# One table for positions, frequencies and norms, and a sum of squares on ScalarE, at the start of a two-layer decoder trunk

## The chip, the cores and the metric

The kernel runs on one core of one Trainium2 chip. The metric is the device time of one execution in microseconds (us); what is compared is the median over several executions.

## The reference, cut to what matters

The reference is a trunk of two residual layers over 256 tokens of width 1024. Layer 0 has gated DeltaNet heads and block attention in parallel, layer 1 has latent attention, and both layers end with a PEER expert network. Each sub-layer starts with the same step, and the attention parts need rotary tables:

```
mod = cond @ mod_w[layer] + mod_b[layer]
sh1, sc1, g1, sh2, sc2, g2 = jnp.split(mod[:, None, :], 6, axis=-1)
h = rmsnorm(x, norm_mix[layer]) * (1.0 + sc1) + sh1
...
inv_freq = ROPE_THETA ** (-jnp.arange(0, dim, 2, dtype=jnp.float32) / dim)
ang = positions.astype(jnp.float32)[..., None] * inv_freq
return jnp.cos(ang), jnp.sin(ang)
```

So before the first product with the input projection `hy_w_in` can run, the kernel needs the sum of squares of each token, 16 columns' worth of `mod` at a time, and the first weights. The rotary tables are needed only later.

## The kernel before, in words

Tokens lie in two tiles of 128 (`TT` = 2), one token per partition. Matrix products run in float32r, each weight and each activation split into a high part (ScalarE, a cast, L132) and a low part (VectorE, a subtraction, L132), three matmuls per pair (L136 to L138).

The change touches the start of `run` (L1673 to L1757). For this stretch the order of SP's DMA issues, of TensorE, VectorE and ScalarE is the order in which the code is written (`in_order`, L1641); only GpSimd is ordered by the scheduler. The steps are:

- SP loads `cond`, the two tiles of `x` (L1677), then, in four rounds `q`, two pieces of the modulation weights `mod0` (`mw`, 1 MB each, L1687) and one piece of `w0start` (`wraw`, 1 MB, L783), the first weights of the input projection. All loads of this stretch go through SP's one queue. In round 0, between the first `mw` and the first `wraw`, stand the small loads: the table `small` with modulation biases and norm gains (L1725), and inside `sincos` (L879), called twice, the frequencies (L888, one DRAM row read for all 128 partitions) and the positions (L889).
- VectorE squares and sums both token tiles (L1714), then runs a chain of tiny operations for the reciprocal root (L202, L154 to L178); ScalarE and VectorE scale the tiles by it (L225, L223) and TensorE transposes them (L232).
- In each round VectorE multiplies modulation weights with the row of `cond` (L349), TensorE does one column of it as 16 one-column matmuls per round (L1693), ScalarE and VectorE split `wraw` (L132), and `quarter` (L276) makes two of the eight 128-row blocks of `hT`, scaled and shifted (L235 to L251). Then the products of that quarter follow (L136 to L138).
- `sincos` runs on GpSimd: positions to float (L891), angles (L893), range reduction (L900 to L909). ScalarE takes the sines much later (L910).

`square_sum` (L192) is an existing helper that squares and sums on ScalarE; later norms use it.

Of the kernel before, what the change touches and what calls it, by code (L numbers as in the profile page):

```python
# [13 lines left out]
I32 = mybir.dt.int32  # L14
U32 = mybir.dt.uint32
AF = mybir.ActivationFunctionType
OP = mybir.AluOpType
AX = mybir.AxisListType

P = 128  # L20
D = 1024
KD = D // P
S = 256
TT = S // P
# [43 lines left out]
class Trunk:  # L68
# [34 lines left out]
    def consts(self):  # L103
        nc, b = self.nc, self.base
        self.x = self.t(b, [P, TT, D])
        self.small = self.t(b, [P, 2 * 48 + 4 * KD])
        self.modb = self.small[:, :96].rearrange("p (l c) -> p l c", l=2)
        self.normc = self.small[:, 96:128].rearrange("p (n c) -> p n c", n=4)
        tmp = ExitStack()
        d = self.t(tmp.enter_context(self.pool("c0", side="right")), [P, P], I32)  # L110
        nc.gpsimd.iota(d, pattern=[[1, P]], base=0, channel_multiplier=-1)
        self.ident = self.t(b, [P, P])
        nc.vector.tensor_scalar(self.ident, d, 0.0, None, op0=OP.is_equal)
        self.causal = self.t(b, [P, P])
        nc.vector.tensor_scalar(self.causal, d, 0.0, NEG, op0=OP.is_gt, op1=OP.mult)
        self.upper = self.t(b, [P, P])
        nc.vector.tensor_scalar(self.upper, d, 0.0, None, op0=OP.is_ge)
        tmp.close()
        self.ones = self.t(b, [P, 1])
        nc.vector.memset(self.ones, 1.0)  # L120
        self.cs1 = self.t(b, [P, TT, 2, 32])
        self.modc = [self.t(b, [P, 48]) for _ in range(2)]
        self.row = self.t(b, [P, D])
        self.ss4, self.ss2 = self.t(b, [P, TT, 4]), self.t(b, [P, TT, 4])
        nc.vector.memset(self.ss4, 0.0)
        self.eps = self.t(b, [P, 4])
        nc.vector.memset(self.eps, RS * EPS / 4)
# [751 lines left out]
    def sincos(self, out, half, freq):  # L879

        nc = self.nc
        tmp = self.t(self.st, [P, D], tag="lo", bufs=2)
        w = TT * half
        ang, t, n, r0, r1 = (tmp[:, k * w:(k + 1) * w].rearrange("p (i f) -> p i f", i=TT) for k in range(5))
        f, pos, posf = (tmp[:, 5 * w + a:5 * w + b]
                        for a, b in ((0, half), (half, half + TT), (half + TT, half + 2 * TT)))
        pos = pos.bitcast(I32)
        nc.sync.dma_start(f, freq[None, :].to_broadcast([P, half]))  # L888
        nc.sync.dma_start(pos, self.a["pos"])  # L889
        ve = nc.gpsimd  # L890
        ve.tensor_copy(posf, pos)  # L891
        for i in range(TT):
            ve.tensor_scalar(ang[:, i], f, posf[:, i:i + 1], None, op0=OP.mult)  # L893
        c1 = 6.28125
        c2 = float((np.float32(2 * np.pi - c1).view(np.uint32) & np.uint32(0xFFFFF000)).view(np.float32))
        c3 = float(2 * np.pi - c1 - c2)
        magic = 12582912.0
        steps = []
        for j, (turn, add) in enumerate(((0.25, float(np.pi / 2)), (0.0, 0.0))):
            ve.tensor_scalar(n, ang, float(0.5 / np.pi), turn, op0=OP.mult, op1=OP.add)  # L900
            ve.tensor_scalar(n, n, magic, None, op0=OP.add)
            ve.tensor_scalar(n, n, -magic, None, op0=OP.add)
            r = (r0, r1)[j]
            for k, c in enumerate((c1, c2, c3)):
                ve.tensor_scalar(t, n, -c, None, op0=OP.mult)
                ve.tensor_tensor(r, t, r if k else ang, op=OP.add)
            lim = 3.1415925
            ve.tensor_scalar(r, r, add, lim, op0=OP.add, op1=OP.min)
            ve.tensor_scalar(r, r, -lim, None, op0=OP.max)  # L909
            steps.append(lambda j=j, r=r: nc.scalar.activation(out[:, :, j], r, AF.Sin))  # L910
        return steps
# [722 lines left out]
    def run(self, out):  # L1634
        nc = self.nc
# [30 lines left out]
        r = Bag()  # L1666
        with self.pool("hc") as hc:
# [7 lines left out]
            nc.sync.dma_start(cond, self.a["condc"])  # L1675
            for i in range(TT):
                nc.sync.dma_start(self.x[:, i], self.a["x"][i * P:(i + 1) * P])  # L1677
            nc.scalar.activation(cond, cond, AF.Silu)
            self.row_of(self.row, cond)
            with self.pool("mod") as mp, start:  # L1680
# [3 lines left out]
                def mods(q, c, pm=None):  # L1684

                    w = self.t(mp, [P, 2, D], tag="mw", bufs=6)
                    nc.sync.dma_start(w, self.a["mod0"][q, c // 8])  # L1687
                    self.mod_tile(0, c, w[:, 0])
                    if pm is None:
                        self.mod_tile(0, c + 1, w[:, 1])  # L1690
                        return
                    for k in range(KD):
                        nc.tensor.matmul(pm[:, c // 8:c // 8 + 1], w[:, 1, k * P:(k + 1) * P], cond[:, k:k + 1],  # L1693
                                         start=k == 0, stop=k == KD - 1)
# [12 lines left out]
                def products(q, cs):  # L1707
                    for c in cs:
                        for j in range(2):
                            product(sums[c], c, j, w, q)  # L1710

                for i in range(TT):
                    sq = self.t(mp, [P, D], tag="sq")
                    nc.vector.scalar_tensor_tensor(sq, self.x[:, i], 1.0, self.x[:, i], op0=OP.mult, op1=OP.mult,  # L1714
                                                   accum_out=self.ss4[:, i, :1])
                e.norm(0, 1)
                e.turn(0, (0,))
                e.turn(1, (0,))
# [1 line left out]
                w = None  # L1720
                for q in range(4):
                    pm = self.ps()
                    mods(q, 8 + 2 * q, pm)
                    if not q:
                        nc.sync.dma_start(self.small, self.a["small"])  # L1725
                        turns = self.sincos(r.cs, 64, self.a["freq_b"]) + self.sincos(self.cs1, 32, self.a["freq_c"])
                    else:
                        products(q - 1, (1, 2, 3))
                    if q < 3:
                        w, steps = self.fetch(self.a["w0start"][q], KD, 256)  # L1730
                        for f in steps:
                            f()
                    mods(q, 2 * q)
                    bias(2 * q)
                    bias(8 + 2 * q, pm)
                    if q == 3:
                        w, steps = self.fetch(self.a["w0start"][q], KD, 256, 4)
                    last = e.quarter(q, tmp)
                    if q < 3:
                        products(q, (0,))  # L1740
                    if q == 1:
                        e.turn(0, (1,))
                        e.turn(1, (1,))
# [58 lines left out]
def _layout(i):  # L1802

    def f(n):
        return np.asarray(i[n])
# [12 lines left out]
    def cols(v):  # L1818
        return v.reshape(v.shape[:-1] + (-1, P)).swapaxes(-1, -2)

    def start(c, natural):
        w = f("mod_w")[0, :, c * P:(c + 2) * P]
        b = w[:, P:]
        return np.stack([w[:, :P].T, b.reshape(KD, P, P).swapaxes(0, 1).reshape(P, -1) if natural else b.T], 1)

    L = 2
    hy = f("hy_w_in")[0]
    wq = f("peer_w_q").reshape(L, KD, P, 8, 256).transpose(0, 3, 2, 1, 4).reshape(L, 8, P, 2048)
    uq = f("mla_w_uq")[0].reshape(512, 8, 192)
# [2 lines left out]
    w0 = chunks(np.concatenate([hy[:, :1536], hy[:, 2056:], hy[:, 1536:2048]], 1), 256)  # L1832
    r = {
        "x": f("x")[0],
        "pos": f("positions")[0].reshape(TT, P).T,
        "modT": f("mod_w").transpose(0, 2, 1),
        "condc": cols(f("c")[0]),
        "mod0": np.stack([np.stack([start(c, c >= 8) for c in (2 * q, 8 + 2 * q)]) for q in range(4)]),
        "small": np.concatenate([cols(f("mod_b")).transpose(1, 0, 2).reshape(P, -1)]
                                + [cols(f(n)[l]) for l in range(L) for n in ("norm_mix", "norm_ffn")], 1),  # L1840
        "w0": w0,
        "w0start": w0[[2, 3, 10, 11]].reshape(4, P, 4, 512).transpose(2, 1, 0, 3).reshape(4, P, 2048),
        "w0ba": one(hy[:, 2048:2056]),
# [11 lines left out]
        "wq": wq,  # L1855
        "keys": f("peer_sub_keys").reshape(L, 16, NK, P).transpose(0, 3, 1, 2),
        "uT": f("peer_u").reshape(L, NK, NK, KD, P).transpose(0, 2, 4, 3, 1).reshape(L, NK, P, D),
        "v": f("peer_v"),
        "final_norm": f("final_norm"),
    }  # L1860
    for n, d in (("freq_b", 128), ("freq_c", 64)):
        r[n] = np.power(np.float32(10000.0), -np.arange(0, d, 2, dtype=np.float32) / np.float32(d)).astype(np.float32)
    return {k: np.ascontiguousarray(v) for k, v in r.items()}


# [15 lines left out]
```

## Time and profile before

| what | value |
|---|---|
| median of 3 runs | 1913.13 us (1910.81 to 1915.3) |
| the profiled execution, its own time | 1913.58 us |
| span of the profile | 1911.8 us |
| TensorE busy | 1878.6 us, 98% of the span |
| VectorE busy | 1532.3 us, 80% |
| ScalarE busy | 943.5 us, 49% |
| GpSimd busy | 48.9 us, 3% |
| mean DMA rate over the span | 196 GB/s |

The profiled execution takes 1.8 us longer than its span; that part lies outside the instructions of the engines. Shares of busy time are averages over the whole span. The change lies in the first 50 us, so the rows that matter are those of that stretch.

### The profile page before, as it was taken

The page shows a single profiled execution, that of the slowest core. Times are in us where ns is not written, and L with a number is a line of the kernel's source. Part 1 is how long each engine was busy: PE and PEld are TensorE (multiplying, and loading weights), DVE is VectorE, ACT ScalarE, POOL GpSimd, SP SyncE. Part 2 cuts the span into 40 slices and gives each one's busy share as a digit, 9 for nine tenths or more (in the row PEclk, how much of TensorE's full clock was granted, in tenths as well). Part 3 has the DMA queues.
Part 4 walks back from the last instruction along what each step waited for, and adds up shares of the span by engine and source line. Part 5 has one row for each costly group of instructions (what it writes and reads, how often), then busy time and mean ns, then how long its engine had stood idle before and what let it go on. Part 6 is the DMA issues. An engine that isn't in the chain of part 4 may idle for free.

```text
span 1911.8 us, 35995 instructions
## 1 busy us (share of the span) xinstructions
PE 1878.6 (98%) x14368; PEld 1722.2 (90%) x14368; DVE 1532.3 (80%) x3265; ACT 943.5 (49%) x1301; POOL 48.9 (3%) x131
## 2 busy tenths in 40 slices
PE   6999999999999999999999999999999999999998
PEld 6999899999999888888889899999999988888886
DVE  7879789999998789865657677999778878985565
ACT  2866555454444444454545754545444444444453
POOL 7001000000000000000000000000000000000000
PEclk9999999999999999999999999999999999999999
DMA  8456475658885555576743455565555555556673
GB/s 324 160 194 214 191 279 187 201 187 284 295 270 187 177 177 177 176 251 195 216 147 111 155 201 175 183 203 186 180 175 170 176 177 176 176 180 199 194 228 103
DMA packets 96504, 374.57 MB, mean 196 GB/s; under 512 B 11856, under 2 KB 12112, under 8 KB 89680
## 3 DMA queue, kind: packets, MB, share of 16 engines
q1 hardware_dynamic: 96336, 372.28, 58.4%
q8 instruction: 112, 1.84, 0.4%
q14 instruction: 56, 0.46, 0.1%
HBM read 371.18 MB, written 1.05 MB: 195 GB/s over the span
## 4 chain that ended last, share of the span: by engine, by line
PE 82%; DVE 9%; DMA 4%; ACT 3%; issue 1%; SPq 0%; ACTq 0%; DVEq 0%
PE ps L776 30%; PE ps L621 21%; PE ps L623 11%; PE ps L136 3%; PE ps L138 3%; PE ps L137 3%; PE ps L644 3%; DVE lo L132 3%; DMA raw<-in_v_dram 2%; PE ps L729 1%; DVE t L349 1%; PE ps L324 1%; ACT hi L132 1%; PE ps L1200 1%; DVE wlo L132 1%
## 5 line engine op out<-in xcount | busy, mean ns | idle before, releaser
L132 ACT CAST hi<-raw 128x1024 fp32r<-128x1024 f32 x508 | 534.8, 1054 | 753.1 <-PE ps L776 310.5
L132 DVE TENSOR_TENSOR lo<-raw,hi 128x1024 fp32r<-128x1024 f32 x508 | 620.0, 1222 | 249.0 <-ACT hi L132 246.8
L621 PE MATMUL ps<-hT,hi 128*128 128x256 f32 x4096 | 514.2, 278 | 0.0
L621 PEld LDWEIGHTS ps<-hT,hi 128*128 128x128 f32 x4096 | 485.8, 188 | 0.2 <-ACT hi L132 0.2
L623 PE MATMUL ps<-hT,lo 128*128 128x256 f32 x2048 | 276.7, 278 | 2.0 <-DVE lo L132 1.9
L776 PE MATMUL ps<-hi,vwh 128*128 128x512 f32 x976 | 266.1, 394 | 1.2 <-ACT hi L132 1.1
L776 PE MATMUL ps<-hi,vwl 128*128 128x512 f32 x976 | 261.3, 389 | 0.0
L776 PE MATMUL ps<-lo,vwh 128*128 128x512 f32 x976 | 260.9, 389 | 0.0
L623 PEld LDWEIGHTS ps<-hT,lo 128*128 128x128 f32 x2048 | 252.4, 188 | 4.1 <-DVE lo L132 3.7
L776 PEld LDWEIGHTS ps<-hi,vwl 128*128 128x128 f32 x976 | 183.2, 188 | 38.8
L776 PEld LDWEIGHTS ps<-lo,vwh 128*128 128x128 f32 x976 | 183.2, 188 | 38.3
L776 PEld LDWEIGHTS ps<-hi,vwh 128*128 128x128 f32 x976 | 180.3, 188 | 38.1 <-ACT hi L132 2.9
L132 DVE TENSOR_TENSOR wlo<-wraw,whi 128x1024 fp32r<-128x1024 f32 (+1 forms) x84 | 99.3, 1202 | 36.1 <-ACT whi L132 36.0
L132 ACT CAST whi<-wraw 128x1024 fp32r<-128x1024 f32 (+1 forms) x84 | 84.3, 1032 | 36.5 <-PE ps L137 14.2
L640 DVE TENSOR_TENSOR ohG<-ohB,t 128x512 f16<-128x512 f16 x256 | 99.3, 418 | 0.0
L136 PE MATMUL ps<-hT,whi 128*128 128x256 f32 x288 | 85.0, 296 | 7.1 <-ACT hT L247 7.1
L634 DVE TENSOR_TENSOR ohA<-t,t 128x1024 f16<-128x1024 f16 x128 | 87.6, 684 | 0.0
L137 PE MATMUL ps<-hT,whi 128*128 128x256 f32 x288 | 83.1, 289 | 0.2 <-DVE hT L251 0.2
L138 PE MATMUL ps<-hT,wlo 128*128 128x256 f32 x288 | 83.1, 289 | 0.0
L644 PE MATMUL ps<-ohG,ohA 128*128 128x64 f16 x2048 | 79.0, 193 | 0.3
L644 PEld LDWEIGHTS <-ohA 128*128 128x128 f16 x2048 | 67.3, 97 | 12.2 <-issue 8.7
L349 DVE SCALAR_TENSOR_TENSOR t<-t,t 128x1024 f32<-128x1024 f32 x56 | 67.4, 1217 | 2.5 <-DMA t<-in_modT_dram 2.5
(478 smaller groups left out, 2251.7 us busy)
## 6 DMA issues: line engine op xcount, KB each, us to landing
raw<-in_uT_dram SPq DMA_DIRECT2D x256, 512.0 KB, 3.3
raw<-in_v_dram SPq DMA_DIRECT2D x256, 512.0 KB, 4.1
t<-in_modT_dram SPq DMA_DIRECT2D x56, 512.0 KB, 5.0
wraw<-in_w_dram SPq DMA_DIRECT2D x13, 1024.0 KB, 6.0
raw<-in_modT_dram SPq DMA_DIRECT2D x24, 512.0 KB, 4.4
wraw<-in_wq_dram SPq DMA_DIRECT2D x12, 1024.0 KB, 5.7
mw<-in_mod_dram SPq DMA_DIRECT2D x8, 1024.0 KB, 13.6
wraw<-in_w0start_dram SPq DMA_DIRECT2D x4, 1024.0 KB, 12.0
```

Of the source, the lines that this page charges most:

```text
L132: return self.nc.scalar.copy(hi, src), self.nc.vector.tensor_sub(lo, src, hi.bitcast(F32))
L136: mm(out, l[0], r[0], start=start, stop=False)
L137: mm(out, l[0], r[1], start=False, stop=False)
L138: mm(out, l[1], r[0], start=False, stop=stop)
L324: mm(ps[g][:, i], e.hT[:, s, k, sl], w[:, b, k, :], start=s + k + b == 0, stop=s == 1 and n == KD - 1)
L349: self.nc.vector.scalar_tensor_tensor(w, w, 1.0, self.row, op0=OP.mult, op1=OP.mult, accum_out=self.modc[layer][:, c:c + 1])
L621: mm(pair, hi[:, k], hT[:, s, k], start=k == 0 and s == 0, stop=False)
L623: mm(pair, lo[:, k], hT[:, 0, k], start=False, stop=k == KD - 1)
L634: nc.vector.tensor_tensor(A, self.iota_t[:, None].to_broadcast(full), pairs(0, full), op=OP.is_equal)
L640: nc.vector.tensor_tensor(B[:, j], b0, pairs(2 + j, part), op=OP.mult)
L644: nc.tensor.matmul(ps[:, t], A[:, t // 2, :, t % 2], B[:, j, t // 2, :, t % 2], start=j == 0, stop=j == 1)
L776: self.nc.tensor.matmul(acc[i][c], w[a][:, j, i * P:(i + 1) * P], v[b][:, c * 512:(c + 1) * 512], start=first and j + a + b == 0, stop=False)
```

## The change

The small table grows from 128 to 226 columns: behind the biases and gains come 64 columns with the frequencies of the first rotary table and 32 with those of the second, written out for each of the 128 partitions on the host, and two columns with the positions (integers whose bits are kept). The table is loaded once, right behind `x`, ahead of the first `mw`. `sincos` reads frequencies and positions from there, and its four loads go. The sum of squares of the second token tile goes from VectorE to ScalarE (`square_sum`); its scratch tile is another one than that of the first tile.

```diff
-        self.small = self.t(b, [P, 2 * 48 + 4 * KD])
+        self.small = self.t(b, [P, 2 * 48 + 4 * KD + 64 + 32 + TT])
...
-        f, pos, posf = (tmp[:, 5 * w + a:5 * w + b]
-                        for a, b in ((0, half), (half, half + TT), (half + TT, half + 2 * TT)))
-        pos = pos.bitcast(I32)
-        nc.sync.dma_start(f, freq[None, :].to_broadcast([P, half]))
-        nc.sync.dma_start(pos, self.a["pos"])
+        f, pos, posf = self.small[:, freq:freq + half], self.small[:, -TT:].bitcast(I32), tmp[:, 5 * w:5 * w + TT]
...
                 nc.sync.dma_start(self.x[:, i], self.a["x"][i * P:(i + 1) * P])
+            nc.sync.dma_start(self.small, self.a["small"])
...
-                for i in range(TT):
-                    sq = self.t(mp, [P, D], tag="sq")
-                    nc.vector.scalar_tensor_tensor(sq, self.x[:, i], 1.0, self.x[:, i], op0=OP.mult, op1=OP.mult,
-                                                   accum_out=self.ss4[:, i, :1])
+                sq = self.t(mp, [P, D], tag="sq")
+                nc.vector.scalar_tensor_tensor(sq, self.x[:, 0], 1.0, self.x[:, 0], op0=OP.mult, op1=OP.mult,
+                                               accum_out=self.ss4[:, 0, :1])
+                self.square_sum(mp, self.ss4[:, 1, :1], self.x[:, 1])
...
-                        nc.sync.dma_start(self.small, self.a["small"])
-                        turns = self.sincos(r.cs, 64, self.a["freq_b"]) + self.sincos(self.cs1, 32, self.a["freq_c"])
+                        turns = self.sincos(r.cs, 64, 128) + self.sincos(self.cs1, 32, 192)
...
         "small": np.concatenate([cols(f("mod_b")).transpose(1, 0, 2).reshape(P, -1)]
-                                + [cols(f(n)[l]) for l in range(L) for n in ("norm_mix", "norm_ffn")], 1),
+                                + [cols(f(n)[l]) for l in range(L) for n in ("norm_mix", "norm_ffn")]
+                                + [np.broadcast_to(freq(d), (P, d // 2)) for d in (128, 64)]
+                                + [f("positions")[0].astype(np.int32).reshape(TT, P).T.view(np.float32)], 1),
```

On SP's queue, the start of the program before (`t_69` is `x`, `t_70` the small table):

```order
L1675 DMA t_106<-in_condc_dram 128x8
L1677 DMA t_69<-in_x_dram 128x1024 x2
L1687 DMA mw_171<-in_mod_dram 128x2048
L1725 DMA t_70<-in_small_dram 128x128
L888 DMA lo_183<-in_freq_b_dram 128x64
L889 DMA lo_183<-in_pos_dram 128x2
L888 DMA lo_211<-in_freq_c_dram 128x32
L889 DMA lo_211<-in_pos_dram 128x2
L783 DMA wraw_239<-in_w0start_dram 128x2048
L1687 DMA mw_247<-in_mod_dram 128x2048
```

The same place now:

```order
L1671 DMA t_106<-in_condc_dram 128x8
L1673 DMA t_69<-in_x_dram 128x1024 x2
L1674 DMA t_70<-in_small_dram 128x226
L1684 DMA mw_172<-in_mod_dram 128x2048
L783 DMA wraw_235<-in_w0start_dram 128x2048
L1684 DMA mw_243<-in_mod_dram 128x2048
```

Five small loads between the first `mw` and the first `wraw` are gone; one, wider, stands in front of the first `mw`.

On VectorE, the norm of both tiles now, with the semaphores that each row waits for (before, a second L1714 with 128x1024 elements stood behind the first, and no row here waited for ScalarE):

```order
L1710 SCALAR_TENSOR_TENSOR sq_127,t_89<-t_69 128x1024 [waits DMAHW1_49,DVE_49]
L202 SCALAR_TENSOR_TENSOR rmsp_133,rmss_26_131<-t_89,t_92 128x4 [waits DVE_49]
L202 SCALAR_TENSOR_TENSOR rmsp_135,rmss_26_131<-t_89,t_92 128x4 [waits DVE_49,Activation_49]
L154 TENSOR_SCALAR rs20y_137<-rmss_26_131 128x2 [waits DVE_49]
L162 TENSOR_SCALAR rs20t_139<-rmss_26_131,rs20y_137 128x1 [waits DVE_49]
```

The second sum, and all behind it, now waits for ScalarE's square, which stands between the copies of `cond` (L345) and the scaling of the tiles (L225). On TensorE nothing moves, and behind this stretch no engine's order moves, GpSimd's share of `sincos` apart, where the two tables are now interleaved from the start.

## Rows read from the trace of the kernel before

**Rows 1.** The page's head and its part on engines: busy us, share of the span, instructions.

```profile
span 1911.8 us, 35995 instructions
PE 1878.6 (98%) x14368; PEld 1722.2 (90%) x14368; DVE 1532.3 (80%) x3265; ACT 943.5 (49%) x1301; POOL 48.9 (3%) x131
```

**Rows 2.** Windows of the start: us, busy us (instructions) of each engine, granted clock, DMA share, GB/s.

```profile
15.50:22.50 7.00, 0.00 (x0) 0.00 (x0) 6.42 (x13) 2.36 (x6) 6.51 (x9) 1.00 1.02 428
25.60:29.00 3.40, 3.40 (x18) 3.40 (x18) 3.40 (x5) 0.00 (x0) 3.32 (x4) 1.00 1.01 417
29.00:34.10 5.10, 5.10 (x24) 5.10 (x25) 4.52 (x13) 3.37 (x6) 4.86 (x8) 1.00 1.00 418
34.10:53.00 18.90, 18.90 (x164) 18.90 (x164) 14.73 (x34) 5.69 (x16) 12.74 (x20) 1.00 0.45 173
...
64.80:71.60 6.80, 6.80 (x33) 6.80 (x33) 5.26 (x23) 5.37 (x9) 0.00 (x0) 0.52 0.81 288
```

**Rows 3.** Chain of work that ended last, 0 to 110 us: start, us, what.

```profile
3.06 0.48 SPq L888
...
4.62 0.43 SPq L889
5.10 9.30 DMA wraw<-in_w0start_dram
```

**Rows 4.** Timeline, 4 to 23.3 us: start, us, engine, line, operation, [idle before <-releaser].

```profile
6.29 1.22 DVE L1714 SCALAR_TENSOR_TENSOR sq<-t 128x1024 f32<-128x1024 f32 x1
...
9.52 1.34 ACT L225 ACTIVATE raw<-t,rmsr 128x512 f32<-128x512 f32 x2 [4.31 <-DVE rmsr L166]
...
10.32 1.22 DVE L349 SCALAR_TENSOR_TENSOR mw<-mw,t 128x1024 f32<-128x1024 f32 x1
...
14.42 1.99 ACT L132 CAST whi<-wraw 128x1024 fp32r<-128x1024 f32 x2 [3.57 <-DMA wraw<-in_w0start_dram]
...
15.50 2.43 DVE L132 TENSOR_TENSOR wlo<-wraw,whi 128x1024 fp32r<-128x1024 f32 x2 [3.96 <-ACT whi L132]
...
22.52 0.58 PE L136 MATMUL ps<-hT,whi 128*128 128x256 f32 x1 [7.06 <-ACT hT L247]
```

**Rows 5.** Windows of one microsecond each, same columns as rows 2.

```profile
8.00:9.00 1.00, 0.00 (x0) 0.00 (x0) 0.96 (x8) 0.00 (x0) 0.00 (x0) 1.00 0.31 81
9.00:10.00 1.00, 0.00 (x0) 0.00 (x0) 1.00 (x6) 0.48 (x1) 0.00 (x0) 1.00 0.15 28
10.00:11.00 1.00, 0.71 (x4) 0.71 (x5) 1.00 (x3) 0.85 (x2) 0.00 (x0) 1.00 0.78 275
11.00:12.00 1.00, 1.00 (x6) 1.00 (x6) 0.54 (x2) 0.00 (x0) 0.54 (x2) 1.00 0.98 402
```

**Rows 6.** DMA view: packets from 8.3 to 9.7 us, and the first `mw` (KB, us to landing).

```profile
DMA packets 120, 0.03 MB, mean 20 GB/s; under 512 B 106, under 2 KB 120, under 8 KB 120
...
mw<-in_mod_dram SPq DMA_DIRECT2D x1, 1024.0 KB, 6.6
```

**Rows 7.** Line 194, squares on ScalarE in layer 1: ns min/median/max, forms.

```profile
L194 ACT ACTIVATE sq<-lat x4: 417/530/633, 1024.1 to 1030.7; 128x256 f32<-128x256 f32 x2, 128x512 f32<-128x512 f32 x2
L194 ACT ACTIVATION_READ_ACCUMULATOR sq<-lat x4: 185/192/204, 1024.4 to 1031.2; 128x1 f32 x4
```

**Rows 8.** Timeline, GpSimd and VectorE beside each other, and ScalarE's sines.

```profile
11.35 0.22 POOL L891 CAST lo<-lo 128x2 f32<-128x2 int32 x1 [10.29 <-DMA lo<-in_pos_dram]
...
13.03 0.54 POOL L901 TENSOR_SCALAR lo<-lo 128x128 f32<-128x128 f32 x1
...
15.43 2.64 POOL L893 TENSOR_SCALAR lo<-lo 128x32 f32<-128x32 f32 x2
...
20.68 0.27 DVE L235 SCALAR_TENSOR_TENSOR hscale<-t,t 128x2 f32<-128x2 f32 x1
...
47.45 0.16 DVE L235 SCALAR_TENSOR_TENSOR hscale<-t,t 128x2 f32<-128x2 f32 x1
...
47.55 0.37 POOL L909 TENSOR_SCALAR lo<-lo 128x64 f32<-128x64 f32 x1
...
51.11 0.80 ACT L910 ACTIVATE t<-lo 128x128 f32<-128x128 f32 x4
```

More of the change, by code (lines that the diff above doesn't have):

```diff
@@ L1824, in start, with freq @@
         return np.stack([w[:, :P].T, b.reshape(KD, P, P).swapaxes(0, 1).reshape(P, -1) if natural else b.T], 1)
+    def freq(d):
+        return np.power(np.float32(10000.0), -np.arange(0, d, 2, dtype=np.float32) / np.float32(d)).astype(np.float32)
     L = 2
@@ L1834, in _layout @@
         "x": f("x")[0],
-        "pos": f("positions")[0].reshape(TT, P).T,
         "modT": f("mod_w").transpose(0, 2, 1),
@@ L1860, in _layout @@
     }
-    for n, d in (("freq_b", 128), ("freq_c", 64)):
-        r[n] = np.power(np.float32(10000.0), -np.arange(0, d, 2, dtype=np.float32) / np.float32(d)).astype(np.float32)
     return {k: np.ascontiguousarray(v) for k, v in r.items()}
```

## The prediction, made before the changed kernel ran

> **What bounds the kernel now.** I read the page's head first: over the whole span TensorE is busy 98% of the time [rows 1], so only what lets TensorE start earlier, or idle less, can shorten the kernel. The change lies in the first 50 us, so I next read the windows of that stretch. From 15.5 to 22.5 us TensorE has no instruction at all; from 25.6 us on its busy time equals the length of every window up to 53 us [rows 2]. It is therefore the start of the first products, at 22.5 us, that sets when the rest runs, and the question is what the start waits for.
>
> The timeline answers it. TensorE's first product ends an idle time of 7.06 us. Before it, ScalarE sat idle for 3.57 us until the first `wraw` had landed, and began to split it at 14.42 us; VectorE's half of the split begins at 15.50 us, after 3.96 us without work [rows 4]. Everything from there to 22.52 us is VectorE work in a row. The chain of waits says the same: it runs along SP's issues, of which four belong to `sincos`, to the `wraw` load of 9.30 us [rows 3]. So **the landing of the first `wraw` bounds the start**; the norm does not, since ScalarE has finished scaling the tiles at 9.52 + 1.34 = 10.86 us and VectorE the first `mw` at 10.32 + 1.22 = 11.54 us [rows 4].
>
> Why does `wraw` land so late? It is issued at 5.10 us. The windows of one microsecond show the DMA engines at 0.31 and 0.15 of their time and 81 and 28 GB/s from 8 to 10 us, and at 0.78 in the next, with 402 GB/s after that [rows 5]. From 8.3 to 9.7 us only 120 packets moved, all under 2 KB, 106 of them under 512 B [rows 6]. That is where the small loads stand in the queue: five loads of 128 rows each, the wide table of 64 KB and the four of `sincos`. There is a hole of (1 - 0.31) + (1 - 0.15) + (1 - 0.78) = 1.76 us of DMA time in front of `wraw`, and no other in reach of it.
>
> **The change part by part.**
>
> The four loads of `sincos` go, and the table, now 226 x 4 x 128 = 116 KB, stands ahead of the first `mw`. The bytes are nearly the same (64 + 32 + 16 + 2 KB before), so what can go is the hole. *Bounds of the gain.* The lower: the hole of 1.76 us, less 0.3 us if the one load that is left makes a hole of its own of a fifth (1.76 / 5 = 0.35): 1.4 us. The upper: the first `mw`, issued at 2.12 us, lands after 6.6 us [rows 6], at 8.7 us; `wraw` lands at 14.4 us, 5.7 us later, and 1 MB at 402 GB/s takes 2.6 us. The excess is 3.1 us, more than the mean hole because the slowest of the 16 engines decides when a load has landed. Less 0.3 us for the table (116 KB at 402 GB/s), that is 2.8 us. I take **2.4 us**, nearer to the upper end, because it is the landing, not the mean, that ScalarE waits for. `wraw` would land at 12.0 us. The loads behind it follow in one stream at 428 GB/s [rows 2], so the second `mw` moves with it.
>
> A page of the Trainium skill looks at this another way: "DMA: Bandwidth & Descriptors", in the section on rules for kernel authors, asks that many small transfers be made one, since under 64 KB one pays mostly overhead, and its table of measured sizes gives 0.68 us for 4 KB and 0.95 us for 64 KB. By that table, as an estimate, four loads of that kind would cost 2.7 to 3.8 us. The trace agrees in sign; its hole of 1.76 us is smaller, since these loads are queued behind each other.
>
> *SP.* Five issues of 0.43 to 0.48 us go from between, one is added ahead: the `wraw` issue moves from 5.10 to about 3.1 us [rows 3]. I cost this at nothing: the DMA engines are still busy with `x` and the first `mw` then, and the queue is never empty. The first `mw` is issued 0.5 us later, behind `x` that is still moving: nothing either.
>
> *The square on ScalarE.* VectorE loses one operation of 1.22 us [rows 4]. ScalarE gains one of 1024 elements: 417 ns at 256 and 633 ns at 512 elements [rows 7], so 0.84 ns per element and about 1.07 us, with 0.19 us to read the sum. Both must wait for the second tile of `x`, which VectorE finds landed at the latest at 6.29 us. So ScalarE would be done at about 7.5 us, where VectorE is done now. Taken as nothing, with bounds of 0.3 us earlier to 0.2 us later; and it is covered by the wait for `wraw`, which at 12.0 us still comes 1.1 us after ScalarE's scaling ends at 10.86. If that cover went, the chain of the norm would be late next.
>
> *GpSimd.* `sincos` starts when the table has landed, behind `x`, at about 6.5 us, not at 11.35 us, and ends 3.2 us before the sines are taken now [rows 8]: (47.55 + 0.37 = 47.92, against 51.11). If it starts 4.8 us earlier and the sines come 2.4 us earlier, the room grows to 5.6 us. Nothing. But GpSimd now works beside VectorE's chain of tiny operations: see the third rival.
>
> *TensorE's clock.* From 29.0 to 34.1 us a product takes 5.10 / 24 = 0.21 us, from 34.1 us on 18.90 / 164 = 0.115 us. In the window from 64.8 to 71.6 us the granted clock reads 0.52, and a product takes 6.80 / 33 = 0.21 us [rows 2]: so the first products run at the lower level, 1.2 GHz, and the column's 1.00 before 34.1 us only means that no change is on record there. The rise came 5.1 us after the one-column matmuls that fill 25.6 to 29.0 us. No row says if it would move with the work. If it stays at 34.1 us, the 2.4 us won are worked off at the lower level and 2.4 x (1 - 0.115 / 0.21) = 1.1 us are given back; if it comes as much earlier as it could stay behind, 1.1 us are won beside. I take nothing, the middle, and keep 1.1 us on both sides.
>
> **The sum.** 1911.8 us of span become 1909.4; with the 1.8 us outside, 1913.6 - 2.4 = 1911.2 us for an execution like the profiled one. That one stands 0.45 us over the median of the three, so for a median **1910.7 us**. TensorE's work behind 22.5 us is not touched, and the loads there are issued when engines free their tiles, so the shift is carried to the end.
>
> **The rivals.**
>
> *The hole stays.* If the gap is not the small loads' own but what the queue does between loads of large rows, the one table ahead of `mw` would make the same gap there, and `wraw` would gain nothing: 1913.1 us. Against it: no such gap is on record between the large loads behind, at 428 GB/s over seven microseconds [rows 2]. For it: the table's rows of 904 bytes are still below 2 KB. This is also the case that the change doesn't do what it says.
>
> *The clock adds to it.* The start comes 2.8 us earlier, the rise another 1.1 us, and the second stretch at 1.2 GHz, 6.8 us that cost 6.8 x 0.46 = 3.1 us, comes out shorter by a third: 2.8 + 1.1 + 1.0 = 4.9 us, 1908.2 us. For it: both stretches lie behind pieces of light work and can shift; against it, they can shift the other way as easily.
>
> *GpSimd holds up VectorE.* From about 6.5 us on, `sincos` runs beside the 13 tiny operations of the norm, two scalings and the first `mw` product: 16 operations on VectorE. If each had to wait for one of GpSimd's, 0.54 us [rows 8], they would end 8.6 us later, at 20.2 instead of 11.54 us, and the split of `wraw` would begin at 20.2 instead of 15.5 us: 4.7 us later than now, 1918 us. It starts to bite where the wait per operation passes 0.1 us (the first half of the split is ready for VectorE at about 13.1, 1.5 us after 11.54) and turns the change into a loss from (15.5 - 11.54) / 16 = 0.25 us. The rows speak against it: beside VectorE's split it is GpSimd whose two small operations take 2.64 us, while the split keeps its 2.43; a tiny operation on VectorE takes 0.27 us beside GpSimd at 20.7 us and 0.16 at another place, 0.11 us more [rows 8]. The Trainium skill has the rule behind this rival ("SBUF — State Buffer", on the side of the engines' ports): VectorE and GpSimd share a pair of ports that one of them holds for a whole instruction, whoever starts first, while the other blocks. By that rule it could go either way; the trace shows mostly GpSimd as the one that blocks.
>
> **How the numbers follow.** Forecast, a gain of 1.4 to 2.8 us with at most 1.1 us of clock either way: 0.68. The hole stays, or the gain is given back: 0.11. The clock adds to it: 0.17. GpSimd holds up VectorE: 0.04. About 0.2%, 3.8 us, is what a measurement of this kernel can tell from no change; the three runs before already spread over 4.5 us. The forecast lies within that bound, 2.4 us, but its upper end, 2.8 + 1.1 = 3.9 us, and the spread of runs push some of it over: of its 0.68 I count 0.08 as faster. With the clock's case that gives faster 0.25; slower 0.04; within 0.2% 0.71. The range reaches from the clock's case, 1908.2 us, to the case without gain, 1913.1, with 0.2 us for the spread: 1908.2 to 1913.3 us.
>
> **What would show it.** Right: in the windows of the changed kernel no microsecond from 3 to 40 us with a DMA share below 0.7; `wraw` landed and ScalarE's split begun at about 12.0 us; TensorE's first product at about 20.1 us; the sines not waiting for GpSimd. Wrong: a new hole near 6 us; ScalarE's split waiting for its own scaling, or VectorE's for the norm, which would mean that the cover has gone; tiny operations of the norm that take twice as long; or a first product 2.4 us earlier and an end that is not, which would send me to TensorE's clock.

## The result, and the profile after

| | median | range | executions |
|---|---|---|---|
| before | 1912.26 us | 1910.81 to 1915.3 | 4 |
| changed | 1943.11 us | 1942.18 to 1946.76 | 4 |

The ratio is 1.0163, with a 95% interval of 1.0144 to 1.0181: the change makes the kernel about 31 us slower. The forecast was 1910.7 us, and its range ended at 1913.3.

The start does what was forecast. The page's head and the timeline of the changed kernel, start and duration in us, then engine, line and operation:

```profile
span 1945.0 us, 35990 instructions
PE 1915.9 (99%) x14368; PEld 1761.2 (91%) x14368; DVE 1533.8 (79%) x3263; ACT 945.7 (49%) x1303; POOL 48.4 (2%) x131
```

```profile
6.35 1.06 ACT L194 ACTIVATE sq<-t 128x1024 f32<-128x1024 f32 x1 [0.88 <-DVE sq L1710]
6.59 0.30 POOL L887 CAST lo<-t 128x2 f32<-128x2 int32 x2 [5.53 <-DMA t<-in_small_dram]
...
9.44 1.33 ACT L225 ACTIVATE raw<-t,rmsr 128x512 f32<-128x512 f32 x2 [1.94 <-DVE rmsr L166]
...
10.34 1.31 DVE L349 SCALAR_TENSOR_TENSOR mw<-mw,t 128x1024 f32<-128x1024 f32 x1
...
12.38 1.99 ACT L132 CAST whi<-wraw 128x1024 fp32r<-128x1024 f32 x2 [1.60 <-DMA wraw<-in_w0start_dram]
13.46 2.60 DVE L132 TENSOR_TENSOR wlo<-wraw,whi 128x1024 fp32r<-128x1024 f32 x2 [1.80 <-ACT whi L132]
...
17.16 1.46 DVE L349 SCALAR_TENSOR_TENSOR mw<-mw,t 128x1024 f32<-128x1024 f32 x1
...
20.75 0.58 PE L136 MATMUL ps<-hT,whi 128*128 128x256 f32 x1 [5.36 <-ACT hT L247]
```

Against [rows 4]: the split of `wraw` begins at 12.38 instead of 14.42 us, 2.04 us earlier, and the first product at 20.75 instead of 22.52, 1.77 us earlier. The hole in the DMA stream [rows 5] is gone; the same microseconds now:

```profile
8.00:9.00 1.00, 0.00 (x0) 0.00 (x0) 1.00 (x7) 0.00 (x0) 0.83 (x4) 1.00 0.99 410
9.00:10.00 1.00, 0.00 (x0) 0.00 (x0) 1.00 (x6) 0.56 (x1) 0.92 (x3) 1.00 1.03 434
```

The loss lies far behind. From 200 us to the end of the span, first before, then changed (columns as in [rows 2]):

```profile
200.00:1911.80 1711.80, 1695.85 (x12977) 1548.68 (x12975) 1368.34 (x2885) 826.35 (x1095) 7.13 (x69) 1.00 0.58 192
```

```profile
200.00:1945.00 1745.00, 1730.85 (x12974) 1585.83 (x12972) 1369.94 (x2880) 827.54 (x1095) 7.13 (x69) 1.00 0.57 188
```

For practically the same 12,970 matmuls TensorE is busy for 35.0 us longer, at a granted clock of 1.00 both times; it does not wait more, it works more slowly. Which matmuls? Two windows of 50 us tell, one in the first product of the PEER network (L621 and L623: the expert weights `uT` times `hT`), one in the second (L776: activations times the expert weights `v`). In each matmul one operand of 128 columns is loaded into TensorE and the other, of 256 or 512 columns, is streamed past it. Before:

```profile
350.00:400.00 50.00, 50.00 (x443) 50.00 (x443) 48.03 (x217) 25.74 (x30) 0.00 (x0) 1.00 0.60 201
850.00:900.00 50.00, 50.00 (x223) 41.40 (x222) 28.41 (x29) 24.58 (x28) 0.00 (x0) 1.00 0.65 201
```

And changed:

```profile
350.00:400.00 50.00, 50.00 (x419) 50.00 (x419) 46.10 (x207) 22.74 (x27) 0.00 (x0) 1.00 0.56 185
850.00:900.00 50.00, 50.00 (x223) 41.40 (x222) 30.37 (x31) 25.54 (x30) 0.00 (x0) 1.00 0.70 228
```

TensorE is full in all four. In the first product 443 matmuls became 419, that is 50 us / 443 = 113 ns each and now 119 ns. In the second nothing changed. The groups of instructions (busy us, mean ns of one with overlap, idle before) add it up; before:

```profile
L621 PE MATMUL ps<-hT,hi 128*128 128x256 f32 x4096 | 514.2, 278 | 0.0
L623 PE MATMUL ps<-hT,lo 128*128 128x256 f32 x2048 | 276.7, 278 | 2.0 <-DVE lo L132 1.9
L776 PE MATMUL ps<-hi,vwh 128*128 128x512 f32 x976 | 266.1, 394 | 1.2 <-ACT hi L132 1.1
```

Changed:

```profile
L621 PE MATMUL ps<-hT,hi 128*128 128x256 f32 x4096 | 537.9, 283 | 0.0
L623 PE MATMUL ps<-hT,lo 128*128 128x256 f32 x2048 | 287.0, 282 | 0.0
L776 PE MATMUL ps<-hi,vwh 128*128 128x512 f32 x976 | 266.2, 394 | 1.5 <-ACT hi L132 1.5
```

L621 and L623 grew by 23.7 + 10.3 = 34.0 us in 6144 matmuls. The span grew by 33.2 us, since the start had won something.

No line of the change touches them. But the table is allocated ahead of `hT`, and growing it by 98 columns (392 bytes, which the allocator rounds up to a multiple of 32) moves `hT` from byte 18080 to byte 18496 of each partition, 416 bytes. The operands that TensorE loads for these products, `hi` (bytes 212960 and 217056) and `lo`, are allocated from the other end and stay. **The theory:** the time of a matmul depends on how far apart in memory the streamed operand (`hT`) and the loaded one (`hi`, `lo`) begin. **The rivals:** the earlier loads, GpSimd beside VectorE, or the square on ScalarE shift the phase of later work; or it is the place of `hT` by itself.

### The profile page after: what moved, and what is told of

Same layout as the page of the kernel before. It is cut to its first block, busy times and chain, and to the rows that moved or that the text cites. A ratio compares the mean times of both kernels' runs of the same rounds, so it can differ in the third digit from the quotient of the medians.

```text
span 1945.0 us, 35990 instructions
## 1 busy us (share of the span) xinstructions
PE 1915.9 (99%) x14368; PEld 1761.2 (91%) x14368; DVE 1533.8 (79%) x3263; ACT 945.7 (49%) x1303; POOL 48.4 (2%) x131
## 4 chain that ended last, share of the span: by engine, by line
PE 88%; DVE 4%; DMA 4%; ACT 3%; issue 1%; SPq 0%; ACTq 0%; DVEq 0%
PE ps L776 31%; PE ps L621 25%; PE ps L623 13%; PE ps L644 3%; PE ps L136 3%; PE ps L138 3%; PE ps L137 3%; DMA raw<-in_v_dram 2%; PE ps L729 1%; PE ps L1196 1%; ACT hi L132 1%; DVE lo L132 1%; DMA raw<-in_wq_dram 1%; PE ps L324 1%; ACT whi L132 1%
## 5 line engine op out<-in xcount | busy, mean ns | idle before, releaser
L621 PE MATMUL ps<-hT,hi 128*128 128x256 f32 x4096 | 537.9, 283 | 0.0
L621 PEld LDWEIGHTS ps<-hT,hi 128*128 128x128 f32 x4096 | 508.2, 188 | 0.0
L623 PE MATMUL ps<-hT,lo 128*128 128x256 f32 x2048 | 287.0, 282 | 0.0
L776 PE MATMUL ps<-hi,vwh 128*128 128x512 f32 x976 | 266.2, 394 | 1.5 <-ACT hi L132 1.5
L623 PEld LDWEIGHTS ps<-hT,lo 128*128 128x128 f32 x2048 | 263.2, 188 | 0.0
L776 PE MATMUL ps<-hi,vwl 128*128 128x512 f32 x976 | 261.3, 389 | 0.0
L776 PE MATMUL ps<-lo,vwh 128*128 128x512 f32 x976 | 260.9, 389 | 0.0
L776 PEld LDWEIGHTS ps<-hi,vwl 128*128 128x128 f32 x976 | 183.2, 188 | 38.8
L776 PEld LDWEIGHTS ps<-lo,vwh 128*128 128x128 f32 x976 | 183.2, 188 | 38.1
L776 PEld LDWEIGHTS ps<-hi,vwh 128*128 128x128 f32 x976 | 180.2, 188 | 38.6 <-ACT hi L132 3.7
L136 PE MATMUL ps<-hT,whi 128*128 128x256 f32 x288 | 86.0, 299 | 5.4 <-ACT hT L247 5.4
L138 PE MATMUL ps<-hT,wlo 128*128 128x256 f32 x288 | 84.2, 293 | 0.0
```

What stands on the lines that cost most here:

```text
L136: mm(out, l[0], r[0], start=start, stop=False)
L138: mm(out, l[1], r[0], start=False, stop=stop)
L621: mm(pair, hi[:, k], hT[:, s, k], start=k == 0 and s == 0, stop=False)
L623: mm(pair, lo[:, k], hT[:, 0, k], start=False, stop=k == KD - 1)
L776: self.nc.tensor.matmul(acc[i][c], w[a][:, j, i * P:(i + 1) * P], v[b][:, c * 512:(c + 1) * 512], start=first and j + a + b == 0, stop=False)
```

## The experiments

### The wide tile without the change, and the change with the distance mended

The first is the kernel before with the wider tile only; every load, every instruction and every order stay.

```diff
-        self.small = self.t(b, [P, 2 * 48 + 4 * KD])
+        self.small = self.t(b, [P, 2 * 48 + 4 * KD + 64 + 32 + TT])[:, :128]
```

> The kernel before with the table's tile made 226 columns wide (904 instead of 512 bytes per partition); loads, queue order and both sums of squares as before, the added columns are never written or read. So every tile laid out behind the table moves by 416 bytes as in the changed kernel, hT from 18080 to 18496, and nothing else changes. Theory A (the changed kernel is slow because the tiles stand elsewhere and TensorE's matmuls that stream hT go from 113 to 120 ns each): 1945 us, L621 and L623 at about 120 ns from start to start, TensorE's share 99%. Rival B (the loads, GpSimd's earlier start or the clock make it slow): 1913 us and 113 ns.

The second is the whole change, with 24 unused columns more, so that `hT` moves by 512 bytes instead of 416.

```diff
-        self.small = self.t(b, [P, 2 * 48 + 4 * KD + 64 + 32 + TT])
+        self.small = self.t(b, [P, 2 * 48 + 4 * KD + 64 + 32 + TT + 24])[:, :226]
```

> The changed kernel with 24 more unused columns behind the table, so that the tiles behind it move by 512 bytes against the kernel before (hT at 18592), not by 416. Theory A, if it is hT's place modulo 512 or a smaller power of two that counts: matmuls back at 113 ns, and the gain of the start that the forecast named is left alone: 1910 to 1912 us. If the place counts modulo 1024 or more, or if rival B holds: 1940 to 1946 us.

Measured: the wide tile alone 1945.86 us, ratio to before 1.0175 (1.0158 to 1.0192); the mended change 1910.52 us against 1913.42 before, ratio 0.9989 (0.9979 to 0.9998). The window of the first product, with the wide tile and then with the mended change:

```profile
350.00:400.00 50.00, 50.00 (x419) 50.00 (x419) 47.01 (x213) 22.89 (x27) 0.00 (x0) 1.00 0.56 184
```

```profile
350.00:400.00 50.00, 50.00 (x443) 50.00 (x442) 47.47 (x208) 27.24 (x32) 0.00 (x0) 1.00 0.61 198
```

The whole loss is there without the change's loads, GpSimd and square, and all of it goes with 96 bytes of padding. The first kind of rival (loads, GpSimd, square) falls.

### Moving either operand

The kernel before, with an unused tile of 104 columns ahead of `hT` (the first), or with one that pushes `hi`, `lo` and all else at that end down by 416 bytes while `hT` stays (the second).

```diff
+        self.t(self.hp, [P, 104])
```

> The kernel before with 416 unused bytes ahead of hT in hT's own pool: hT and the pools above it move by 416 bytes, all tiles below hT (x, the table, the row of cond, the norms' tiles) stay. Theory A with hT as the tile that counts: 1945 us and 120 ns per matmul of L621. If it is one of the small tiles below hT: 1913 us.

```diff
+        self.t(self.ctx.enter_context(self.pool("gap", side="right")), [P, 104])
         self.st = self.ctx.enter_context(self.pool("st", side="right"))
```

> The kernel before with 416 unused bytes above the pool of hi, lo and raw, which moves them down by 416 bytes (hi from 212960 to 212544) and with them the weights' pools below; hT stays at 18080. The distance between the streamed hT and the loaded hi is then that of the changed kernel. Theory A1 (the distance of TensorE's two operands counts): 120 ns per matmul of L621 and about 1945 us. Theory A2 (hT's own place counts): 113 ns and about 1913 us, unless the moved weights have a price of their own in L776, which streams vwh and vwl and is at 227 ns now.

Measured, one execution each: 1945.12 and 1945.93 us, and 419 matmuls in the window both times. With the weights moved it reads:

```profile
350.00:400.00 50.00, 50.00 (x419) 50.00 (x419) 46.98 (x213) 22.88 (x27) 0.00 (x0) 1.00 0.56 184
```

The place of `hT` by itself is not it: it did not move here. (The expectation of this run names the operands of L776 the wrong way round: `hi` and `lo` are streamed there, `vwh` and `vwl` loaded.)

### Eight places, and both operands moved

The kernel before, with an unused tile of 8, 16 or 64 columns (32, 64 or 256 bytes) ahead of `hT`:

```diff
+        self.t(self.hp, [P, 8])
```

> The kernel before with hT 32 bytes further (18112), the loaded weights hi and lo where they were. Theory C (what counts is the distance of hT and hi/lo modulo 64: 0 before and in e2, 32 in the changed kernel, e1, e3 and e4): 120 ns per matmul of L621 and about 1945 us. Theory D (a larger period, 128 to 512 bytes, with 416 and 96 bytes off as bad places): 113 ns and 1913 us, or something between.

> The kernel before with hT 64 bytes further (18144). Theory C (distance modulo 64): 113 ns and about 1913 us. Theory D (a larger period): anything else, up to 120 ns and 1945 us.

> The kernel before with hT 256 bytes further (18336). Theory C (distance modulo 64): 113 ns and about 1913 us. Theory D (a period of 512 or more): other than 113 ns.

In the next one `hT` goes up by 32 bytes and `hi` and `lo` down by 480, so that the distance changes by 512.

```diff
+        self.t(self.hp, [P, 8])
+        self.t(self.ctx.enter_context(self.pool("gap", side="right")), [P, 120])
         self.st = self.ctx.enter_context(self.pool("st", side="right"))
```

> The kernel before with hT 32 bytes further (18112) and hi and lo 480 bytes lower (hi at 212480): both now start at a multiple of 64, as neither did before, and their distance is 512 bytes more, 0 modulo 64. Theory C (the distance alone): 113 ns per matmul of L621 and about 1913 us. If the place of either one by itself counts beside the distance: other than 113 ns.

And the places that were left, by 24, 32, 48 and 56 columns:

> The kernel before with hT 96 bytes further. Theory C (modulo 64) has fallen: +32 gave 117 ns, +64 gave 120, +256 and +512 gave 114. Theory E: the distance of hT and hi counts modulo 256. Then +416 of the changed kernel is +160, and the map so far is 0: 113, 32: 117, 64: 120, 160: 120. By E a place between 64 and 160 is slow as well: 120 ns, about 1945 us. Theory F, a period of 128: +96 is fast or as +32, 113 to 117 ns.

> The kernel before with hT 128 bytes further. Theory E (period 256): the middle of the slow places, 120 ns, about 1945 us. Theory F (period 128): 113 ns, about 1913 us.

> The kernel before with hT 192 bytes further, that is 64 bytes short of a full 256. Theory E (period 256) with slow places that are symmetric about +112: 114 to 118 ns. Should the place before not be the best one, this or +224 can be below 113 ns: then up to 30 us less than before.

> The kernel before with hT 224 bytes further, 32 bytes short of 256. Theory E (period 256): 113 to 117 ns; 113 if the fast places are wide on this side, 117 if they are symmetric about the place before.

Measured, one execution each (the kernel before took 1909.37 us beside the runs with 32, 64 and 256 bytes and both moved, and 1916.08 us beside those with 96, 128, 192 and 224). So single times are rough, and the columns to read are the last two: the matmuls of the window from 350 to 400 us, and the busy time of the group L621.

| distance changed by, bytes | modulo 256 | time, us | matmuls in 50 us | L621, us |
|---|---|---|---|---|
| 0 (before) | 0 | | 443 | 514.2 |
| 256 | 0 | 1914.23 | 443 | 516.0 |
| 512 (both moved) | 0 | 1915.22 | 444 | 514.9 |
| 32 | 32 | 1936.56 | 425 | 532.0 |
| 64 | 64 | 1945.77 | 419 | 538.4 |
| 96 | 96 | 1927.71 | 431 | 526.9 |
| 128 | 128 | 1932.0 | 427 | 529.4 |
| 416 (the change) | 160 | | 419 | 537.9 |
| 192 | 192 | 1941.12 | 424 | 534.8 |
| 224 | 224 | 1934.71 | 428 | 530.9 |

Both distances in the table that differ from that of before by a multiple of 256 bytes are as quick as before, and the other seven lose between 13 and 24 us in L621 alone. The windows with `hT` alone up by 32 bytes, and with `hi` and `lo` moved as well, so that the distance fits again:

```profile
350.00:400.00 50.00, 50.00 (x425) 50.00 (x424) 48.29 (x222) 22.05 (x26) 0.00 (x0) 1.00 0.56 187
```

```profile
350.00:400.00 50.00, 50.00 (x444) 50.00 (x443) 48.77 (x217) 25.57 (x30) 0.00 (x0) 1.00 0.60 198
```

The first costs time, the second costs none. So it is the distance, and the good place comes back after 256 and after 512 bytes; that a bad place costs the same 256 bytes further on was not tried. A period of 64 or of 128 bytes falls. The allocator of this kernel goes in steps of 32 bytes, so these are all eight places that an unused tile can reach (160 by way of 416): the place of before is the best, and no other is near it. How the loss depends on the seven others is irregular, and why is open.

The profiles of these runs hold two more groups of products that say the same. L136 to L138, the trunk's own products, stream `hT` against loaded weights in some places and stream the weights against a loaded `hT` in others. Count from the start of the streamed operand to the start of the loaded one, modulo 256. Where `hT` is streamed this is 64 before, as in L621, and the median time from one start to the next, behind 90 us, is 114 ns before, 120 ns with 64 bytes ahead of `hT` and 118 ns with 128 bytes; L621 and L623 read 113, 120 and 118 ns. Where `hT` is loaded the count is 192 before, and the median 118 ns; with 128 bytes ahead of `hT` the count becomes 64, and the median 114 ns, the lowest of all eight places. So the sign of the distance matters too, and these products stood at a bad place in the kernel before.

One rival was not tried by a run: ScalarE and VectorE write the next `hi` and `lo` meanwhile, at the same distance modulo 256 from `hT`, and might be what hinders TensorE. The profiles speak against it. From one start to the next in L621 and L623, the mean rose from 114.4 to 120.0 ns where ScalarE was idle and VectorE busy, from 116.0 to 122.1 ns where both were busy, and from 117.4 to 122.5 ns where only ScalarE was (before and changed).

### The other product

If distance matters, L776 should feel it too. Its operands lie at the same end, a multiple of 256 bytes apart (8192 for the first `hi` and `vwh`), and none of the kernels above changed that. The mended change, with an unused tile of 64, 32 or 128 bytes between `hi` and `vwh`, and a gap that makes it up to 256 bytes for `hi` and `lo`, so that the first product keeps its good place:

```diff
+        if not tags and "vpad" not in self.__dict__:
+            self.__dict__["vpad"] = self.t(self.st, [P, 16])
...
+        self.t(self.ctx.enter_context(self.pool("gap", side="right")), [P, 48])
         self.st = self.ctx.enter_context(self.pool("st", side="right"))
```

> The realigned change, with a tile of 64 bytes between hi and vwh, so that the two operands of the second PEER product (L776: hi or lo streamed in 512 columns, vwh or vwl loaded) lie 64 bytes further apart; hT stays at a fast distance from hi. If the distance acts on every fp32r product, L776 changes its mean pitch of 227 ns and with 2928 such matmuls the time moves by 2.9 us per ns; if the loss is one ns in sixteen as in the first product, by up to 40 us. If the distance acts only on products whose operands are in pools at the two ends of the memory, or only on 256-column products, the pitch stays at 227 ns and the time at that of the realigned change, about 1910.5 us.

> As the run before, with 32 bytes instead of 64. If distance acts on L776 too, its pitch differs from 227 ns and from that at 64 bytes; if not, the same three numbers as in the realigned change: L776 at 227 ns, L621 at 113 ns, about 1910.5 us.

> As the run before, with 128 bytes. If distance acts on L776 too, its pitch differs from 227 ns; a lower one would be the first place better than that of the kernel before, and the time would fall by 2.9 us per ns. If not, about 1910.5 us.

Measured: 1926.89, 1926.06 and 1925.16 us, ratios to before 1.0070 (1.0050 to 1.0089), 1.0071 (1.0049 to 1.0092) and 1.0068 (1.0048 to 1.0087). With 64 bytes the windows and one of the three groups (L778 is L776, two lines further down) read:

```profile
350.00:400.00 50.00, 50.00 (x443) 50.00 (x443) 47.47 (x209) 27.22 (x32) 0.00 (x0) 1.00 0.59 200
850.00:900.00 50.00, 50.00 (x216) 40.30 (x215) 28.55 (x28) 23.55 (x27) 0.00 (x0) 1.00 0.60 196
```

```profile
L778 PE MATMUL ps<-hi,vwh 128*128 128x512 f32 x976 | 271.2, 399 | 0.0
```

The mended change reads in the second window:

```profile
850.00:900.00 50.00, 50.00 (x222) 41.45 (x221) 27.52 (x28) 24.73 (x29) 0.00 (x0) 1.00 0.62 199
```

The first product is as before, 443. The second has 216 matmuls in 50 us where the mended change has 222: 231 instead of 225 ns. The other two give 216 as well. So the distance matters in both products, and here too the place of before was the best of the four seen. It is not the same place: the loaded operand begins 194880 bytes behind the streamed one in the first product, 64 modulo 256, and 8192 bytes behind it in the second, 0 modulo 256; for the second, 64 is a bad place. No single good distance follows for all products. **The cost at the worst places is about 6 ns for a matmul of 256 streamed columns, and at the three places tried also about 6 ns for one of 512.** Each of them comes with one load of 128 columns, so the cost goes with the matmul and its load, not with the number of columns streamed. A load and a stream that hinder each other would fit; that is not shown, since no kernel here streams without loading.

### The two halves of the change

What the mended change gained was split: its loads with both squares on VectorE, and the square on ScalarE alone in the kernel before.

```diff
-                sq = self.t(mp, [P, D], tag="sq")
-                nc.vector.scalar_tensor_tensor(sq, self.x[:, 0], 1.0, self.x[:, 0], op0=OP.mult, op1=OP.mult,
-                                               accum_out=self.ss4[:, 0, :1])
-                self.square_sum(mp, self.ss4[:, 1, :1], self.x[:, 1])
+                for i in range(TT):
+                    sq = self.t(mp, [P, D], tag="sq")
+                    nc.vector.scalar_tensor_tensor(sq, self.x[:, i], 1.0, self.x[:, i], op0=OP.mult, op1=OP.mult,
+                                                   accum_out=self.ss4[:, i, :1])
```

> The change with the 24 unused columns (operands 512 bytes further apart than before, the fast distance), and the squares of both token tiles on VectorE again: only the loads differ from before. If the gain of the change lies in the loads, as the prediction has it (the landing of the first wraw): the split of wraw begins at 12.4 us as in the changed kernel (14.4 before), the first product at 20.8 to 21.0 us (22.5 before), and the time is 1.5 to 3 us below the kernel before (ratio 0.9984 to 0.9992). If the square on ScalarE is needed for it (VectorE's second square holds up the norm, and the norm now bounds the start): the first product at 21.5 us or later and a gain below 1 us.

The square alone is the same edit the other way round, in the kernel before.

> Before with the square of the second token tile on ScalarE, and nothing else; all tiles stay where they are. By the prediction the norm is covered by the wait for the first wraw, so the split still begins at 14.4 us, the first product at 22.5 us, and the time is that of before (ratio 0.9995 to 1.0005). By the rival, that the norm's chain bounds VectorE's part of the split, the first product comes up to 0.9 us earlier and the time falls by as much (ratio 0.9995 or below).

Measured: the loads alone 1910.08 us against 1913.44 before, ratio 0.9979 (0.9969 to 0.9990); the square alone 1911.82 us, ratio 0.9993 (0.9984 to 1.0002), which is not told apart from nothing. Timeline of the loads alone, then of the square alone:

```profile
12.11 1.99 ACT L132 CAST whi<-wraw 128x1024 fp32r<-128x1024 f32 x2 [1.28 <-DMA wraw<-in_w0start_dram]
...
20.41 0.58 PE L136 MATMUL ps<-hT,whi 128*128 128x256 f32 x1 [4.97 <-ACT hT L247]
```

```profile
14.47 1.99 ACT L132 CAST whi<-wraw 128x1024 fp32r<-128x1024 f32 x2 [3.83 <-DMA wraw<-in_w0start_dram]
...
22.37 0.58 PE L136 MATMUL ps<-hT,whi 128*128 128x256 f32 x1 [7.13 <-ACT hT L247]
```

The gain of the start is the loads', 2.1 us at the first product and 3.4 us at the median; with the square alone `wraw` lands where it did before, though ScalarE's scaling of the tiles begins at 9.29 instead of 9.52 us. The loads alone at the good distance are the best version found: they beat the kernel before by 0.1 to 0.3%, and the mended change, with its square, is not told apart from them.

## Why the prediction was wrong, point by point

*The step that failed.* "TensorE's work behind 22.5 us is not touched, and the loads there are issued when engines free their tiles, so the shift is carried to the end." The sum took the span of before and subtracted 2.4 us, which carries every duration behind 22.5 us over unchanged. The instructions were indeed untouched, but their operands were not: the wider tile moved `hT`, and 6144 matmuls took 34.0 us longer. The diff showed the tile growing by 98 columns; the text counted its bytes as a transfer and not as a shift of what is allocated behind it. No row of before has an operand at another place, so the trace could not price it; but a bound on the slow side was owed, and the only one given, GpSimd against VectorE with a chance of 0.04, was of another kind. One sign of being wrong did come out, "a first product 2.4 us earlier and an end that is not"; but it would have sent its reader to TensorE's clock, and that reads 1.00 behind 200 us in both kernels.

Two pages of the Trainium skill bear on this step. "SBUF — State Buffer", in the section on who interferes with whom, says that the ports which VectorE and GpSimd share are the only place of contention, and that TensorE waits for nobody. "TensorE: Matmul & The Clock Gate", in the step-by-step section, adds that loading the next weights takes no bandwidth from the running matmul. The runs show that the same matmul takes 113 or 119 ns by the place of its operands; here the measurement decides.

*The landing of `wraw`: right.* Forecast 12.0 us; measured 12.38 with the change, 12.11 with the loads alone. The term of 2.4 us came out at 2.04 and 2.31. That the landing bounds the start is shown by the square alone, which ends the norm earlier and leaves the landing at 14.47 us.

*The first product: nearly right.* Forecast about 20.1 us; measured 20.75, and 20.41 for the loads alone. Between the landing and the product 0.27 us were lost: VectorE's split took 2.60 instead of 2.43 us and the second `mw` product 1.46 instead of 1.30. GpSimd works beside both, but so it did before, with other operations of `sincos`; with the loads alone the split takes 2.40 us and the two `mw` products 1.47 and 1.33 us. So it is argued and not shown that GpSimd lengthens them. The third rival itself did not come: the small operations of the norm, with GpSimd beside them now, keep their 0.33 and 0.46 us, and nothing like its 8.6 us was lost.

*The square: right.* ScalarE ends it at 6.35 + 1.06 + 0.19 = 7.60 us for 7.5 forecast, and ScalarE's scaling ends at 9.44 + 1.33 = 10.77 us, 1.6 us before `wraw` has landed.

*GpSimd's tables: right.* Its last operation and the sines stand in the timeline so:

```profile
40.63 1.36 POOL L905 TENSOR_SCALAR lo<-lo 128x64 f32<-128x64 f32 x1
...
49.56 0.80 ACT L906 ACTIVATE t<-lo 128x128 f32<-128x128 f32 x4
```

The room is 49.56 - 41.99 = 7.6 us, 5.6 forecast.

*The hole stays: this rival fell,* by the windows from 8 to 10 us above. The lowest DMA share of any microsecond from 3 to 40 us is 0.82, where the prediction asked for at least 0.7.

*The clock: not decided, and not a matter of the start.* The stretch at half clock is still there with the change, a little earlier:

```profile
64.80:71.60 6.80, 6.80 (x37) 6.80 (x38) 5.58 (x21) 4.22 (x8) 0.00 (x0) 0.58 0.74 268
```

In the profile of the square alone, whose start hardly differs from that of before, the same window reads:

```profile
64.80:71.60 6.80, 6.78 (x57) 6.57 (x57) 6.29 (x27) 4.81 (x8) 0.00 (x0) 1.00 0.89 289
```

57 matmuls instead of 33 before [rows 2], at a full clock. The prediction took this stretch as a property of the kernel. It comes and goes between executions of one and the same kernel. For 43 executions of the kernel before, the mean granted clock of the span is on record: 19 read 0.996 or 0.997, as do all seven profiles that have the whole stretch, and 24 read 0.998 or 0.999, as do the other profiles. The 19 took 2.4 us longer in the mean, 1914.7 against 1912.3 us. So the stretch, priced at 3.1 us and larger than the gain that was forecast, belongs to the spread of the runs, and the one profile of before happened to have it.

The rise of the clock after the first products, for which the prediction kept 1.1 us on both sides, neither stayed at its time nor followed the work. By the traces it came at 34.3 us before, at 32.9 with the change, 31.6 with the mended change, 30.0 with the loads alone and 33.0 with the square alone; in the twelve profiles whose start is that of before it came between 25.6 and 35.1 us. At the prediction's price of 0.46 us for each microsecond at the lower level, that alone is a spread of 4.4 us between single executions, where the allowance was 2.2 us from end to end.

*The sum, with the distance mended:* forecast 2.4 us of gain, measured 2.9 us at the median, and 0.02 to 0.21% by the interval, which is 0.4 to 4.0 us. The mechanism of the start was right; what stood behind the sum was not. How near it came to the forecast is partly luck, since the interval is wider than the forecast itself.

## What to carry to other kernels

A tile that grows moves every tile allocated behind it, and a change of the start can so set the speed of matmuls a millisecond later. When a time moves by more than the change can explain, count matmuls per window in stretches that it does not touch, then make the same kernel with the tile padded and nothing else. Where TensorE is the bound, try the eight places of 32 bytes for the streamed operand against the loaded one, for each product that counts, and pin the good one, so that later edits cannot undo it.

## What was not expected of the hardware

- The distance from the streamed to the loaded operand of a float32r matmul, modulo 256 bytes, decides between 113 and 116 to 119 ns per matmul (256 columns streamed) and between 225 and 231 ns (512 columns). With 256 columns one place of eight is good, 64, whichever of the two tiles is streamed; with 512 columns, of four places seen, 0 is good, and 32, 64 and 128 are not.
- The stretch at half clock at 60 to 75 us was wholly there in 7 of 19 profiles, partly in one and absent in 11, with the granted clock of that window at 0.77, 0.89 and 1.00. Among the kernels that differ from before by nothing but an unused tile, 32 bytes of it had the stretch and 64 bytes had not; by the mean clock it also comes and goes between executions of the kernel before.
